# Written MLP order of a two-layer decoder trunk: another ring for the fourth weight piece, the first product copied ahead of the next step's splits, the turned blocks split ahead of two weight pieces

## The chip, the cores and the metric

The kernel runs on one core of one Trainium2 chip, as one program. The metric is device time in microseconds (us). TensorE (PE in the profile) multiplies, VectorE (DVE) and ScalarE (ACT) do the elementwise work, GpSimd (POOL) and SyncE (SP) mostly issue DMAs here.

## The reference

Two decoder layers over 256 tokens of width 2048, batch 1, everything in float32. Each layer has a token mixer and memory attention, and ends with a squared-ReLU MLP of inner width 8192:

```python
hm = _rmsnorm(x, g_mlp[i])
x = x + jnp.square(jax.nn.relu(hm @ w_mlp1[i])) @ w_mlp2[i]
```

The change touches the MLP alone. `w_mlp1` is 2048 x 8192 and `w_mlp2` is 8192 x 2048, both float32, so each layer reads 134 MB of MLP weights.

## The kernel before

**Exact products by halves.** TensorE multiplies in fp32r. Every weight and activation is split into a high part (ScalarE, `activation Copy` into fp32r, line 114) and a low part (VectorE, source minus high part, line 115). A product is three matmuls: high x high, high x low, low x high (`passes`, lines 606 to 608).

**How the MLP is tiled.** The 8192 inner columns are eight chunks `c` of 1024. The up projection of a chunk is done as a fast 2x2 block product with seven products (`p1` to `p7`, of which the trace prints only the letter `p`) instead of eight. It takes eight *steps* `kp`, each over 256 of the 2048 rows. A step loads two 512 KB pieces, `b` and `o` (lines 221 and 223), forms their sums on VectorE (`s` at line 226, then lines 230 and 232 overwrite halves of `o`), splits them into `bh/bl`, `oh`, `sh/sl`, `th/tl`, and runs 7 x 3 = 21 matmuls. After step 7, `end_up(c)` copies the first product out of PSUM (`c1`, line 655; the trace calls it `t`), combines the seven sums on VectorE into four blocks `u` (lines 656 to 664) and squares them on ScalarE (lines 611 and 612).

`to_hT(c)` turns the four blocks on TensorE (line 677, tile `pu`) and splits them into `hT`. `group_down(c, n, t)` is then 24 matmuls into `psd`, over eight pieces `dw`; the four 512 KB weight loads of one `n` (named by `k` = 0, 2, 4, 6) serve the two groups `t` = 0 and 1. `add_down` scales `psd` into `part` (line 699) and adds it to `x_sb` in SBUF by an accumulating GpSimd DMA (line 700).

**What sets the order.** The MLP loop stands inside `tc.manual_schedule()`: on each engine, instructions run in the order in which the Python emits them. For chunk `c` and `g` = 0 to 7 the loop emits: the matmuls of step `g`+1 of chunk `c+1` (for `g` = 7: of step 0 of chunk `c+2`); the loads and splits of the step after that one (`prep`); for odd `g`, loads and splits of the first two weight pieces of the next `n` (`prep_down(*more, (0,))`); a down group; its `add_down`; for odd `g`, the last two pieces (`prep_down(*more, (1,))`). At `g` = 0, `to_hT(c)` is interleaved with the step's products: block, `p1`, block, `p3` and `p2`, block, `p5` and `p7`, block, `p6` and `p4`. At `g` = 6, `end_up(c+1)` is emitted after `prep`.

**Rings.** All weight loads go through SP's one in-order queue; a load waits there until its buffer is free, and everything behind it waits too. The `raw` ring for down weights has three buffers (`RAW = 3`), so the fourth piece of an `n` waits until the first piece of the same `n` is split. The `ux` ring for `b` and `o` has five (`UX = 5`), of which two steps take four. The split pieces of a step have seven buffers (`UP = 7`), one step's worth, so ScalarE can start splitting for a step only when TensorE has used the same piece of the step before.

**PSUM.** Eight banks. A chunk's seven products hold seven of them until `end_up` has read them. The `pu` blocks and the `psd` groups share the eighth, one after the other.

Of the kernel before, what the change touches and what calls it, by code (L numbers as in the profile page):

```python
# [9 lines left out]
F32 = mybir.dt.float32  # L10
# [3 lines left out]
AF = mybir.ActivationFunctionType  # L14
# [3 lines left out]
P = 128  # L18
# [16 lines left out]
UX = 5  # L35
UT = 2
UP = 7
RAW = 3
# [20 lines left out]
def trunk(ctx: ExitStack, tc: tile.TileContext, x, mem, g_attn, w_in, w_out, lambda_qk,  # L59
          subln_g, g_mem, w_mem_kv, g_mlp, w_mlp1, w_mlp2, g_final, out):  # L60
    nc = tc.nc
# [3 lines left out]
    wpool = ctx.enter_context(tc.tile_pool(name="wpool", bufs=3))  # L65
    apool = ctx.enter_context(tc.tile_pool(name="apool", bufs=10))
    upool = ctx.enter_context(tc.tile_pool(name="upool", bufs=1))
# [4 lines left out]
    def bank(shape, nm, gemm=False):  # L72

        return psum.tile(shape, F32, tag="m" if gemm else "a", name=nm)
# [1 line left out]

    x_sb = const.tile([P, 2, D], F32, name="x_sb")

    def load_weights(src, k, c, nm):

        raw = wpool.tile([P, 1024], F32, tag="raw", bufs=RAW, name=f"raw_{nm}")
        nc.sync.dma_start(raw.rearrange("p (k c) -> p k c", c=c), src.rearrange("(k p) c -> p k c", p=P))
        return raw

# [28 lines left out]
    def split(dst_hi, dst_lo, src):  # L113
        nc.scalar.activation(dst_hi, src, AF.Copy)  # L114
        nc.vector.tensor_tensor(dst_lo, src, dst_hi.bitcast(F32), op=ALU.subtract)  # L115

    def weights(src, k, c, nm, raw=None):

        if raw is None:
            raw = load_weights(src, k, c, nm)  # L120
        hi = wpool.tile([P, 1024], F32R, tag="whi", bufs=WH, name=f"hi_{nm}")
        lo = wpool.tile([P, 1024], F32R, tag="wlo", bufs=WH, name=f"lo_{nm}")
        split(hi, lo, raw)
        return [(hi[:, kk * c:(kk + 1) * c], lo[:, kk * c:(kk + 1) * c]) for kk in range(k)]

    def gemm_feat(w, acts, nm, raws=(None,) * 4):

        ps = [bank([P, 2, 256], f"ps_{nm}_{j}", True) for j in range(2)]
        for pc in range(4):
            wt = weights(w[pc * 512:(pc + 1) * 512, :], 4, 256, f"{nm}_{pc}", raws[pc])  # L130
            for kk in range(4):
                k = 4 * pc + kk
                hi, lo = wt[kk]
                a = acts[k // 4][:, k % 4]
                for j in range(2):
                    last = k == KT - 1
                    cols = slice(j * P, (j + 1) * P)

                    def low(**f):
                        nc.tensor.matmul(ps[j][:, 0, :], lo[:, cols], a[:, 0, :], **f)  # L140

                    def high(**f):
                        nc.tensor.matmul(ps[j].rearrange("p h t -> p (h t)"), hi[:, cols], a.rearrange("p h t -> p (h t)"), **f)  # L143

                    if last:
                        low(start=False, stop=False)
                        high(start=False, stop=True)
                    else:
                        high(start=(k == 0), stop=False)
                        low(start=False, stop=False)  # L150
        return ps
# [14 lines left out]
    def act_tile(nm):  # L166
        return apool.tile([P, 4, 2, S], F32R, tag="act", name=nm)
# [270 lines left out]
    for i in range(DEPTH):  # L438
# [12 lines left out]
        for c in range(2):  # L451
            f0 = 3 * MIXW + c * 256
            ps = ps_first if i == c == 0 else gemm_feat(wi[:, f0:f0 + 256], xT, f"qm{i}{c}")
# [16 lines left out]
        for pr in range(NH // 2):  # L470
            ps = gemm_feat(wi[:, pr * 256:(pr + 1) * 256], xT, f"q{i}{pr}")
# [3 lines left out]
            ps = gemm_feat(wi[:, MIXW + pr * 256:MIXW + (pr + 1) * 256], xT, f"k{i}{pr}")  # L475
            aT2 = upool.tile([P, 2, 384], F32, tag="up", bufs=UP, name=f"aT{i}{pr}")
            feat_scaled(kT, ps, 1.0, rowb, f"k{i}{pr}")
            for j in range(2):
                h = 2 * pr + j
                nm = f"{i}_{h}"  # L480
# [99 lines left out]
        for c in range(4):  # L580
            ps = [bank([P, 512], f"pso{i}{c}_{t}", True) for t in range(2)]
            for n, g in enumerate(("m", 0, 1, 2)):
                r0 = MIXW if g == "m" else g * 512
# [13 lines left out]
        NC = DFF // 1024  # L597
# [7 lines left out]
        def passes(ps, acts, hi, lo, first, last):  # L605
            nc.tensor.matmul(ps, acts[:, 0, :], hi, start=first, stop=False)  # L606
            nc.tensor.matmul(ps, acts[:, 0, :], lo, start=False, stop=False)  # L607
            nc.tensor.matmul(ps, acts[:, 1, :], hi, start=False, stop=last)  # L608

        def squared(u, src, sign):  # L610
            nc.scalar.activation(u, src, AF.Relu, scale=sign)
            nc.scalar.activation(u, u, AF.Square)
# [16 lines left out]
        banks, facts, dw = {}, {}, {}  # L629
# [9 lines left out]
        def step_up(c, kp, turns=None, prep=None):  # L639

            if kp == 0:
                banks[c] = {n: bank([P, 512], f"{n}_{i}{c}", n in ("p1", "p2", "p5", "p7")) for n in facts[c, 0]}
            for n, (hi, lo) in facts.pop((c, kp)).items():
                if turns and n in ("p1", "p3", "p5", "p6"):
                    next(turns)
                    if n in ("p1", "p5"):
                        next(prep)
                passes(banks[c][n], comb[kp][:, FACTORS.index(n)], hi, lo, kp == 0, kp == KP - 1)

        def end_up(c):  # L650

            nm, ps = f"{i}{c}", banks.pop(c)
            c1, u2, u3, u4 = (work.tile([P, 512], F32, tag="tmp", bufs=TMP, name=f"t{n}_{nm}") for n in range(4))
            c11, m12, c21, m22 = (work.tile([P, 512], F32, tag="ev", bufs=EV, name=f"u{n}_{nm}") for n in range(4))
            nc.scalar.activation(c1, ps["p1"], AF.Copy)  # L655
            nc.vector.tensor_tensor(c11, c1, ps["p2"], op=ALU.add)
            nc.vector.tensor_tensor(u2, c1, ps["p6"], op=ALU.subtract)
            squared(c11, c11, 1.0)
            nc.vector.tensor_tensor(u4, u2, ps["p5"], op=ALU.add)
            nc.vector.tensor_tensor(m12, u4, ps["p3"], op=ALU.add)  # L660
            squared(m12, m12, -1.0)
            nc.vector.tensor_tensor(u3, u2, ps["p7"], op=ALU.add)
            nc.vector.tensor_tensor(m22, u3, ps["p5"], op=ALU.add)
            nc.vector.tensor_tensor(c21, u3, ps["p4"], op=ALU.add)
            yield
            squared(m22, m22, -1.0)
            squared(c21, c21, 1.0)
            ublk[c] = ((c11, 0, 0), (m12, 0, 1), (c21, 1, 0), (m22, 1, 1))

        def to_hT(c):  # L670

            for f in range(2):
                hT[f] = act_tile(f"hT{i}{c}{f}")
            for n, (u, t, f) in enumerate(ublk[c]):
                pt = bank([P, 4, P], f"pu_{i}{c}{n}")
                for k in range(4):
                    nc.tensor.transpose(pt[:, k], u[:, k * P:(k + 1) * P], ident)  # L677
                cols = slice(t * P, (t + 1) * P)
                split(hT[f][:, :, 0, cols], hT[f][:, :, 1, cols], pt)
                yield  # L680

        def prep_down(c, n, halves):

            for h in halves:
                for k in (4 * h, 4 * h + 2):
                    r0 = c * 1024 + k * P
                    dw[c, n, k], dw[c, n, k + 1] = weights(w_mlp2[i][r0:r0 + 256, n * 512:(n + 1) * 512], 2, 512,
                                                           f"d{i}{c}{n}{k}")

        def group_down(c, n, t, gemm):  # L690

# [34 lines left out]
        def run(steps):  # L726
            for _ in steps:
                pass

        up_plain()  # L730
        with tc.manual_schedule():
            run(prep_up(1, 0))
            step_up(1, 0)
            run(prep_up(1, 1))
            prep_down(0, 0, (0, 1))
            for c in range(NC - 1):
                for g in range(8):
                    uc, kp = (c + 1, g + 1) if g < 7 else (c + 2, 0)
                    pc, pk = (c + 1, g + 2) if g < 6 else (c + 2, g - 6)
                    prep = prep_up(pc, pk) if pc < NC else iter(())  # L740
                    if g == 0:
                        step_up(uc, kp, to_hT(c), prep)
                    elif uc < NC:
                        step_up(uc, kp)
                    run(prep)
                    ending = end_up(c + 1) if g == 6 else iter(())
                    next(ending, None)
                    n, t = g // 2, g % 2
                    more = (c, n + 1) if n < 3 else (c + 1, 0)
                    if t == 1:  # L750
                        prep_down(*more, (0,))
                    add_down(c, n, t, group_down(c, n, t, False))
                    run(ending)
                    if t == 1:
                        prep_down(*more, (1,))
            run(to_hT(NC - 1))
        last_down(NC - 1)
        xT = nxt
# [6 lines left out]
    for f in range(2):  # L765
        r0 = DFF - 1024 + f * 512
# [61 lines left out]
```

## Time and profile before

| | us |
|---|---|
| median of 3 runs (lowest, highest) | 2529.24 (2524.58, 2531.04) |
| the profiled execution | 2528.95 |
| its span, first to last instruction | 2527.2 |

| engine | busy us | share of the span |
|---|---|---|
| TensorE, matmuls | 2262.8 | 90% |
| VectorE | 1718.1 | 68% |
| ScalarE | 1334.0 | 53% |
| GpSimd | 115.8 | 5% |

The profile gives one execution. Its page has the busy share in 40 slices of the span; the trace behind it can be asked for the instructions of one engine in order of time (each with the idle time before it and what ended that), for the sum of waits by who waited for whom, and for the busy time and granted TensorE clock of any stretch. The two MLP loops run from about 518 to 1270 us and from about 1717 to 2470 us. A matmul's printed duration is its latency; matmuls overlap, so the distance between two starts is what one costs.

### The profile page before, as it was taken

Reading aid. Unit: us, or ns where it says so; the run is one execution under the profiler, and the core shown is the slowest. Engines: PE = TensorE matmul, PEld = TensorE weight load, DVE = VectorE, ACT = ScalarE, POOL = GpSimd, SP = SyncE. Lnnn points to the kernel's source line nnn. Section 1 sums busy time; section 2 is a strip of 40 time slices with the busy share of each in tenths; the row PEclk is TensorE's granted clock in tenths of the full one; section 3 lists DMA queues with packets and bytes.
Section 4 is the critical chain, followed back from the end, with each engine's and each line's share of the span. In section 5 each row is a group of like instructions: output and inputs, shape, how many; then the busy total and the mean of one; then the engine's idle time right before and its main releaser. Section 6 shows DMA issues by size and latency. Waiting matters only on the chain.

```text
span 2527.2 us, 28282 instructions
## 1 busy us (share of the span) xinstructions
PE 2262.8 (90%) x10358; PEld 1842.7 (73%) x10358; DVE 1718.1 (68%) x2084; ACT 1334.0 (53%) x1840; POOL 115.8 (5%) x146
## 2 busy tenths in 40 slices
PE   9999999988879788797999999998787978879797
PEld 7888887866757566575778888886675756657676
DVE  6567766667677677676766655766767767767675
ACT  7455554645455555555555544554545555555554
POOL 0000000000000000000000000000000000000000
PEclk9999999999989889898999999999998989989899
DMA  7655555645655565654655556564565556565465
GB/s 236 191 175 167 160 179 174 186 151 157 197 171 166 164 196 156 192 180 150 187 163 187 167 175 192 183 187 149 158 195 167 167 158 200 154 191 183 150 193 161
DMA packets 262397, 443.48 MB, mean 175 GB/s; under 512 B 14497, under 2 KB 80242, under 8 KB 262002
## 3 DMA queue, kind: packets, MB, share of 16 engines
q1 hardware_dynamic: 245856, 412.14, 50.5%
q0 software_dynamic: 16128, 29.37, 6.5%
q8 instruction: 81, 1.33, 0.2%
q14 instruction: 58, 0.48, 0.1%
q10 hardware_dynamic: 274, 0.17, 0.0%
HBM read 409.12 MB, written 3.15 MB: 163 GB/s over the span
## 4 chain that ended last, share of the span: by engine, by line
PE 53%; DVE 16%; DMA 16%; ACT 7%; issue 7%; SPq 1%; DVEq 0%; ACTq 0%; POOL 0%; POOLq 0%
DMA o<-in_w_mlp_dram 11%; DVE bl L115 4%; DMA raw_d<-in_w_mlp_dram 4%; PE ps_q L143 4%; PE ps_k L143 4%; ACT th L114 4%; PE psd L606 3%; PE psd L608 3%; PE psd L607 3%; DVE lo_d L115 3%; PE p L607 3%; PE p L606 2%; PE p L608 2%; PE pso L163 2%; PE pso L164 2%
## 5 line engine op out<-in xcount | busy, mean ns | idle before, releaser
L115 DVE TENSOR_TENSOR lo_d<-raw_d,hi_d 128x1024 fp32r<-128x1024 f32 x252 | 300.3, 1222 | 241.0 <-ACT hi_d L114 240.7
L606 PE MATMUL psd<-hi_d,hT 128*128 128x512 f32 x1008 | 395.5, 393 | 10.3 <-ACT hT L114 9.9
L607 PE MATMUL psd<-lo_d,hT 128*128 128x512 f32 x1008 | 394.2, 391 | 0.0
L608 PE MATMUL psd<-hi_d,hT 128*128 128x512 f32 x1008 | 393.2, 391 | 0.0
L114 ACT ACTIVATE hi_d<-raw_d 128x1024 fp32r<-128x1024 f32 x252 | 260.1, 1051 | 220.4 <-DMA raw_d<-in_w_mlp_dram 213.6
L606 PEld LDWEIGHTS psd<-hi_d,hT 128*128 128x128 f32 x1008 | 190.0, 189 | 56.8 <-ACT hT L114 11.4
L114 ACT ACTIVATE th<-o 128x1024 fp32r<-128x1024 f32 x112 | 118.8, 1061 | 196.7 <-DVE o L232 175.8
L608 PEld LDWEIGHTS psd<-hi_d,hT 128*128 128x128 f32 x1008 | 189.9, 188 | 40.4 <-DVE hT L115 0.6
L607 PEld LDWEIGHTS psd<-lo_d,hT 128*128 128x128 f32 x1008 | 190.2, 189 | 39.0
L226 DVE TENSOR_TENSOR s<-b,o 128x1024 f32<-128x1024 f32 x112 | 136.9, 1222 | 90.6 <-DMA o<-in_w_mlp_dram 90.6
L115 DVE TENSOR_TENSOR bl<-b,bh 128x1024 fp32r<-128x1024 f32 x112 | 136.8, 1221 | 87.8 <-ACT bh L114 87.8
L606 PE MATMUL p<-bh,cb_xm 128*128 128x512 f32 x224 | 105.1, 469 | 70.4 <-ACT t L655 66.6
L700 POOL DMA_DIRECT2D x_sb<-part x112 | 97.4, 869 | 1495.2 <-ACT part L699 1495.2
L677 PE MATMUL pu<-ident,u 128*128 128x128 f32 x256 | 50.8, 338 | 128.0 <-DVE hT L115 101.9
L677 PEld LDWEIGHTS pu<-ident,u 128*128 128x128 f32 x256 | 36.6, 172 | 149.3 <-DVE hT L115 114.7
L114 ACT ACTIVATE sh<-s 128x1024 fp32r<-128x1024 f32 x112 | 118.5, 1058 | 46.1 <-DVE s L226 39.7
L115 DVE TENSOR_TENSOR tl<-o,th 128x1024 fp32r<-128x1024 f32 x112 | 137.2, 1225 | 5.9 <-ACT th L114 0.3
L114 ACT ACTIVATE bh<-b 128x1024 fp32r<-128x1024 f32 x112 | 118.2, 1055 | 39.0 <-DMA b<-in_w_mlp_dram 32.8
L143 PE MATMUL ps_q<-xT,hi_q 128*128 128x512 f32 x384 | 138.4, 401 | 0.0
L143 PE MATMUL ps_k<-xT,hi_k 128*128 128x512 f32 x384 | 138.0, 399 | 0.0
L115 DVE TENSOR_TENSOR sl<-s,sh 128x1024 fp32r<-128x1024 f32 x112 | 136.5, 1218 | 0.0
L607 PE MATMUL p<-bl,cb_xm 128*128 128x512 f32 x224 | 100.0, 446 | 31.3 <-DVE bl L115 31.3
(331 smaller groups left out, 5174.7 us busy)
## 6 DMA issues: line engine op xcount, KB each, us to landing
raw_d<-in_w_mlp_dram SPq DMA_DIRECT2D x252, 512.0 KB, 9.1
b<-in_w_mlp_dram SPq DMA_DIRECT2D x112, 512.0 KB, 9.1
o<-in_w_mlp_dram SPq DMA_DIRECT2D x112, 512.0 KB, 9.9
x_sb<-part POOLq DMA_DIRECT2D x112, 256.0 KB, 5.3
raw_q<-in_w_in_dram SPq DMA_DIRECT2D x48, 512.0 KB, 3.7
raw_k<-in_w_in_dram SPq DMA_DIRECT2D x48, 512.0 KB, 3.6
raw_v<-in_w_in_dram SPq DMA_DIRECT2D x48, 512.0 KB, 3.7
raw_o<-in_w_out_dram SPq DMA_DIRECT2D x48, 512.0 KB, 3.7
```

The lines of the kernel that those rows point to most:

```text
L114: nc.scalar.activation(dst_hi, src, AF.Copy)
L115: nc.vector.tensor_tensor(dst_lo, src, dst_hi.bitcast(F32), op=ALU.subtract)
L143: nc.tensor.matmul(ps[j].rearrange("p h t -> p (h t)"), hi[:, cols], a.rearrange("p h t -> p (h t)"), **f)
L163: nc.tensor.matmul(ps[t], ah, lo, start=False, stop=False)
L164: nc.tensor.matmul(ps[t], al, hi, start=False, stop=last and kk == 3)
L226: nc.vector.tensor_tensor(s, b, o[:, 0:1].to_broadcast([P, 2, 512]), op=ALU.add)
L606: nc.tensor.matmul(ps, acts[:, 0, :], hi, start=first, stop=False)
L607: nc.tensor.matmul(ps, acts[:, 0, :], lo, start=False, stop=False)
L608: nc.tensor.matmul(ps, acts[:, 1, :], hi, start=False, stop=last)
L677: nc.tensor.transpose(pt[:, k], u[:, k * P:(k + 1) * P], ident)
L700: nc.gpsimd.dma_start(x_sb[:, t, n * 512:(n + 1) * 512], part, accum_op=ALU.add)
```

## The change

Three edits, in the MLP's written order and its loads. `load_weights` can take its buffer from the `ux` ring, and `prep_down` does so for the piece `k` = 6. `end_up` gives control back right after the copy `c1`, and the loop calls that part before `prep`. At `g` = 7 the last two weight pieces of the next chunk are no longer prepared after the group; they are prepared at the next `g` = 0, after the step and its `to_hT`. The same holds ahead of the first chunk.

```diff
-    def load_weights(src, k, c, nm):
-
-        raw = wpool.tile([P, 1024], F32, tag="raw", bufs=RAW, name=f"raw_{nm}")
+    def load_weights(src, k, c, nm, other=False):
+
+        if other:
+            raw = upool.tile([P, 1024], F32, tag="ux", bufs=UX, name=f"raw_{nm}")
+        else:
+            raw = wpool.tile([P, 1024], F32, tag="raw", bufs=RAW, name=f"raw_{nm}")
...
             c1, u2, u3, u4 = (work.tile([P, 512], F32, tag="tmp", bufs=TMP, name=f"t{n}_{nm}") for n in range(4))
+            nc.scalar.activation(c1, ps["p1"], AF.Copy)
+            yield
             c11, m12, c21, m22 = (work.tile([P, 512], F32, tag="ev", bufs=EV, name=f"u{n}_{nm}") for n in range(4))
-            nc.scalar.activation(c1, ps["p1"], AF.Copy)
...
-                    dw[c, n, k], dw[c, n, k + 1] = weights(w_mlp2[i][r0:r0 + 256, n * 512:(n + 1) * 512], 2, 512,
-                                                           f"d{i}{c}{n}{k}")
+                    w, nm = w_mlp2[i][r0:r0 + 256, n * 512:(n + 1) * 512], f"d{i}{c}{n}{k}"
+                    dw[c, n, k], dw[c, n, k + 1] = weights(w, 2, 512, nm, load_weights(w, 2, 512, nm, k == 6))
...
-            prep_down(0, 0, (0, 1))
+            prep_down(0, 0, (0,))
...
                     if g == 0:
                         step_up(uc, kp, to_hT(c), prep)
+                        prep_down(c, 0, (1,))
                     elif uc < NC:
                         step_up(uc, kp)
+                    ending = end_up(c + 1) if g == 6 else iter(())
+                    next(ending, None)
                     run(prep)
-                    ending = end_up(c + 1) if g == 6 else iter(())
                     next(ending, None)
...
-                    if t == 1:
+                    if t == 1 and n < 3:
                         prep_down(*more, (1,))
+            prep_down(NC - 1, 0, (1,))
             run(to_hT(NC - 1))
```

ScalarE, layer 0, at `g` = 6 of chunk 4. `hi_d` are the last two weight pieces of `n` = 3, `t<-p` is the copy `c1`, and `bh`, `oh`, `sh`, `th` are the splits for step 0 of chunk 6. Before:

```order
L114 ACTIVATE hi_d_8105<-raw_d_8103 128x1024
L114 ACTIVATE hi_d_8111<-raw_d_8109 128x1024
L114 ACTIVATE bh_8143<-b_8136 128x1024
L114 ACTIVATE oh_8141<-o_8138 128x512
L114 ACTIVATE sh_8151<-s_8140 128x1024
L114 ACTIVATE th_8155<-o_8138 128x1024
L655 ACTIVATE t_05_8159<-p_05_7478 128x512
L611 ACTIVATE u_05_8163<-u_05_8163 128x512
```

The copy stands behind the four splits. After:

```order
L117 ACTIVATE hi_d_8105<-raw_d_8103 128x1024
L117 ACTIVATE hi_d_8111<-raw_d_8109 128x1024
L657 ACTIVATE t_05_8136<-p_05_7478 128x512
L117 ACTIVATE bh_8148<-b_8141 128x1024
L117 ACTIVATE oh_8146<-o_8143 128x512
L117 ACTIVATE sh_8156<-s_8145 128x1024
L117 ACTIVATE th_8160<-o_8143 128x1024
L614 ACTIVATE u_05_8164<-u_05_8164 128x512
```

The copy stands ahead of them; nothing else moved here.

VectorE, layer 0, around `to_hT(5)`. `lo_d` are the low parts of the four weight pieces of the next `n` = 0, `hT` the low parts of the four turned blocks, `s` and `bl` belong to the next step. Before:

```order
L115 TENSOR_TENSOR lo_d_7532<-raw_d_7529,hi_d_7531 128x1024
L115 TENSOR_TENSOR lo_d_7538<-raw_d_7535,hi_d_7537 128x1024
L115 TENSOR_TENSOR lo_d_7572<-raw_d_7569,hi_d_7571 128x1024
L115 TENSOR_TENSOR lo_d_7578<-raw_d_7575,hi_d_7577 128x1024
L115 TENSOR_TENSOR hT_7581<-pu_7583,hT_7581 128x4x128
L226 TENSOR_TENSOR s_7594<-b_7590,o_7592 128x1024
L115 TENSOR_TENSOR hT_7582<-pu_7600,hT_7582 128x4x128
L115 TENSOR_TENSOR hT_7581<-pu_7613,hT_7581 128x4x128
L115 TENSOR_TENSOR bl_7621<-b_7590,bh_7620 128x1024
L115 TENSOR_TENSOR hT_7582<-pu_7630,hT_7582 128x4x128
L230 TENSOR_TENSOR o_7592<-s_7594,b_7590 128x512
```

All four weight pieces stand ahead of the first turned block. After:

```order
L118 TENSOR_TENSOR lo_d_7532<-raw_d_7529,hi_d_7531 128x1024
L118 TENSOR_TENSOR lo_d_7538<-raw_d_7535,hi_d_7537 128x1024
L118 TENSOR_TENSOR hT_7569<-pu_7571,hT_7569 128x4x128
L229 TENSOR_TENSOR s_7582<-b_7578,o_7580 128x1024
L118 TENSOR_TENSOR hT_7570<-pu_7588,hT_7570 128x4x128
L118 TENSOR_TENSOR hT_7569<-pu_7601,hT_7569 128x4x128
L118 TENSOR_TENSOR bl_7609<-b_7578,bh_7608 128x1024
L118 TENSOR_TENSOR hT_7570<-pu_7618,hT_7570 128x4x128
L118 TENSOR_TENSOR lo_d_7634<-raw_d_7631,hi_d_7633 128x1024
L118 TENSOR_TENSOR lo_d_7640<-raw_d_7637,hi_d_7639 128x1024
L233 TENSOR_TENSOR o_7580<-s_7582,b_7578 128x512
```

Two pieces now stand behind the turned blocks, and ahead of the rest of the step's sums.

SP's queue at the same kind of place (the next `n` = 0 of chunk 2). `raw_d` are the weight pieces, `b` and `o` a step's. Before:

```order
L82 DMA raw_d_6063<-in_w_mlp_dram 128x2x512
L82 DMA raw_d_6069<-in_w_mlp_dram 128x2x512
L82 DMA raw_d_6103<-in_w_mlp_dram 128x2x512
L82 DMA raw_d_6109<-in_w_mlp_dram 128x2x512
L221 DMA b_6124<-in_w_mlp_dram 128x2x512
L223 DMA o_6126<-in_w_mlp_dram 128x2x512
```

After:

```order
L85 DMA raw_d_6063<-in_w_mlp_dram 128x2x512
L85 DMA raw_d_6069<-in_w_mlp_dram 128x2x512
L224 DMA b_6112<-in_w_mlp_dram 128x2x512
L226 DMA o_6114<-in_w_mlp_dram 128x2x512
L85 DMA raw_d_6165<-in_w_mlp_dram 128x2x512
L85 DMA raw_d_6171<-in_w_mlp_dram 128x2x512
```

Two step loads pass two weight loads there. Everywhere else in the loop SP's order is the same, and what differs is the buffer that the fourth piece goes to: before it took the buffer of the first piece of its own `n`, now one that was last read a pair of steps earlier. The loads of `b` and `o` now also wait for readers one pair of steps earlier (`bh` on ScalarE and `tl` on VectorE). TensorE's order in the loop is unchanged.

## Rows read from the trace of the kernel before

**Rows 1.** The page: busy time by engine.

```profile
PE 2262.8 (90%) x10358; PEld 1842.7 (73%) x10358; DVE 1718.1 (68%) x2084; ACT 1334.0 (53%) x1840; POOL 115.8 (5%) x146
```

**Rows 2.** Stretches: start and end, length, busy time by engine (with instructions), granted TensorE clock, DMA share, GB/s. The first is one period of the loop in layer 0, from one start of step `g` = 6 to the next, the second the stage between the two MLPs, the last two six such periods of each layer.

```profile
815.40:924.20 108.80, 91.20 (x377) 72.36 (x376) 78.97 (x84) 57.86 (x70) 6.93 (x8) 0.92 0.57 174
1278.00:1720.00 442.00, 439.57 (x2264) 373.07 (x2262) 266.44 (x359) 231.77 (x363) 1.41 (x2) 1.00 0.57 174
...
599.10:1250.00 650.90, 545.01 (x2257) 432.69 (x2256) 470.40 (x499) 344.61 (x414) 41.56 (x48) 0.91 0.57 175
1798.00:2450.00 652.00, 547.51 (x2255) 434.38 (x2254) 469.93 (x498) 344.50 (x414) 41.64 (x48) 0.91 0.57 174
```

**Rows 3.** TensorE in order of time (start, duration, tile, idle time before and what ended it): one `to_hT` and the first matmul of the first group, then the first matmul of steps `g` = 1, 2 and 6, then the next `to_hT` (of the first `to_hT` the first, third and fourth block are shown, of the next the first).

```profile
847.18 0.66 PE L677 MATMUL pu<-ident,u 128*128 128x128 f32 x4 [1.83 <-ACT part L699]
...
858.51 0.66 PE L677 MATMUL pu<-ident,u 128*128 128x128 f32 x4
...
860.59 0.66 PE L677 MATMUL pu<-ident,u 128*128 128x128 f32 x4
...
862.67 0.50 PE L606 MATMUL psd<-hi_d,hT 128*128 128x512 f32 x1
...
868.24 0.39 PE L606 MATMUL p<-bh,cb_xm 128*128 128x512 f32 x1
...
878.44 0.39 PE L606 MATMUL p<-bh,cb_xm 128*128 128x512 f32 x1
...
924.25 0.39 PE L606 MATMUL p<-bh,cb_xm 128*128 128x512 f32 x1
...
955.77 0.66 PE L677 MATMUL pu<-ident,u 128*128 128x128 f32 x4 [1.50 <-ACT part L699]
```

**Rows 4.** Who TensorE waited for in the one period of rows 2 (total us, times, longest).

```profile
PE pu L677 <- DVE hT L115: 6.7, 1, 6.7
PE p L606 <- ACT t L655: 6.0, 1, 6.0
PE p L607 <- DVE bl L115: 2.2, 1, 2.2
PE pu L677 <- ACT part L699: 1.8, 1, 1.8
```

**Rows 5.** SP's queue in order of issue over one pair of steps (a row that is merged, x4, spans from its first to its last issue).

```profile
877.40 0.37 SPq L82 DMA_DIRECT2D raw_d<-in_w_mlp_dram  x1
...
880.12 20.88 SPq L82 DMA_DIRECT2D raw_d<-in_w_mlp_dram  x4
```

**Rows 6.** What ScalarE and VectorE waited for over six periods of layer 0 (599 to 1250 us).

```profile
ACT hi_d L114 <- DMA raw_d<-in_w_mlp_dram: 84.4, 24, 4.5
...
DVE s L226 <- DMA o<-in_w_mlp_dram: 40.7, 24, 3.0
```

**Rows 7.** VectorE in order of time: the end of one pair's weight pieces, and then `g` = 6 (the fourth piece, the next step's first sum, two of the `u` operations).

```profile
876.15 2.35 DVE L115 TENSOR_TENSOR lo_d<-raw_d,hi_d 128x1024 fp32r<-128x1024 f32 x2
...
930.41 1.23 DVE L115 TENSOR_TENSOR lo_d<-raw_d,hi_d 128x1024 fp32r<-128x1024 f32 x1 [3.06 <-ACT hi_d L114]
934.35 1.23 DVE L226 TENSOR_TENSOR s<-b,o 128x1024 f32<-128x1024 f32 x1 [2.71 <-DMA o<-in_w_mlp_dram]
...
941.56 0.68 DVE L657 TENSOR_TENSOR t<-t,p 128x512 f32<-128x512 f32 x1
...
943.60 0.68 DVE L662 TENSOR_TENSOR t<-t,p 128x512 f32<-128x512 f32 x1
```

**Rows 8.** ScalarE in order of time at `g` = 6 of the same chunk (third and fourth weight piece, copy `c1`), and then the fourth piece ahead of the last `to_hT` of layer 0.

```profile
925.04 1.05 ACT L114 ACTIVATE hi_d<-raw_d 128x1024 fp32r<-128x1024 f32 x1
929.32 1.06 ACT L114 ACTIVATE hi_d<-raw_d 128x1024 fp32r<-128x1024 f32 x1 [3.23 <-DMA raw_d<-in_w_mlp_dram]
...
939.69 0.58 ACT L655 ACTIVATE t<-p 128x512 f32<-128x512 f32 x1
...
1271.06 1.06 ACT L114 ACTIVATE hi_d<-raw_d 128x1024 fp32r<-128x1024 f32 x1 [3.23 <-DMA raw_d<-in_w_mlp_dram]
```

**Rows 9.** DMA issues on the page: line, count, size, median us from issue to landing, of the MLP's three loads and of one that comes in the stage between the MLPs.

```profile
raw_d<-in_w_mlp_dram SPq DMA_DIRECT2D x252, 512.0 KB, 9.1
...
o<-in_w_mlp_dram SPq DMA_DIRECT2D x112, 512.0 KB, 9.9
...
raw_q<-in_w_in_dram SPq DMA_DIRECT2D x48, 512.0 KB, 3.7
```

**Rows 10.** The first `to_hT` of layer 0, TensorE and VectorE in order of time: first block, VectorE's first three weight pieces, second block, the first matmul of the first group, and that of step `g` = 6 of that chunk.

```profile
517.77 0.60 PE L677 MATMUL pu<-ident,u 128*128 128x128 f32 x4
...
521.23 3.49 DVE L115 TENSOR_TENSOR lo_d<-raw_d,hi_d 128x1024 fp32r<-128x1024 f32 x3
...
530.54 1.12 PE L677 MATMUL pu<-ident,u 128*128 128x128 f32 x4 [11.48 <-DVE hT L115]
...
538.06 0.50 PE L606 MATMUL psd<-hi_d,hT 128*128 128x512 f32 x1
...
599.10 0.39 PE L606 MATMUL p<-bh,cb_xm 128*128 128x512 f32 x1
```

**Rows 11.** Two stretches of 3 us, after the burst of issues that begins in rows 5 and later in the same pair (columns as in rows 2; the last is GB/s).

```profile
889.00:892.00 3.00, 2.43 (x12) 1.69 (x11) 2.92 (x5) 1.46 (x2) 0.00 (x0) 1.00 1.03 390
895.00:898.00 3.00, 3.00 (x15) 2.49 (x14) 2.97 (x5) 1.00 (x2) 0.00 (x0) 1.00 0.14 24
```

## The prediction

> **What bounds the kernel now.** I began with the busy shares [rows 1]: TensorE is at 90% and no other engine above 68%, but that is a mean over stages. By stretches [rows 2], TensorE has no idle time worth naming between the two MLPs (439.57 of 442 us, clock 1.00). In an MLP period of 108.8 us it is busy 91.2 us and its clock is granted at 0.92. So the loss lies in the MLP loops: six periods take 650.9 us in layer 0 and 652.0 us in layer 1.
>
> How little could a period take? A step with its group is 45 matmuls, and the starts of steps 1 and 2 are 878.44 - 868.24 = 10.20 us apart with no wait between [rows 3], or 0.227 us a matmul: 4.76 us a step, 5.44 us a group. Eight are 81.6 us, and the four turned blocks add about 2 (estimate: 0.66 us each [rows 3], partly overlapped). That is 83.6 us. VectorE has 79.0 us of work in the period and ScalarE 57.9 [rows 2], so TensorE is the floor, with VectorE close behind it.
>
> Who does TensorE wait for [rows 4]? 6.7 us for the low part of the first turned block, 6.0 us for the copy `c1`, 2.2 us for `bl`, and 1.8 us for `part`: 16.7 us. The other 108.8 - 83.6 - 16.7 = 8.5 us agree with the clock: 8% of 108.8 us is 8.7 us, lost at the lower of the two levels, 1.2 instead of 2.4 GHz.
>
> All four waits are late elementwise work, and the queue and the two elementwise engines show why it is late [rows 5 to 8]. SP issues the fourth weight piece at 877.40 us [rows 5], just as the low part of that group's first piece ends (876.15 plus half of 2.35 us [rows 7]); the next fourth piece, last of the merged row, goes out at 880.12 + 20.88 - 0.37 = 900.63. A pair of steps thus takes 23.2 us, against 20.4 us of matmuls. ScalarE waits for a weight DMA 24 times in six periods, 84.4 us in all, and VectorE for the step's `o`, queued behind it on SP, 24 times, 40.7 us [rows 6]. That is once in each pair. The elementwise engines lose three to five us on TensorE there, and it pays at `c1` and at `to_hT`.
>
> **The fourth piece in the steps' ring.** It goes to a buffer last read one pair earlier, so SP no longer stops in mid-pair. The price is that `b` and `o` now wait for readers one pair earlier. On a 20.4 us pair the latest of these, `o` of an odd step, is free after the low part `tl` of that step and wanted when VectorE forms `s` for the same step of the next pair. Setting the row durations one behind the other gives some 12.6 us between (estimate). The loads land 9.1 to 9.9 us after issue in today's bursts, 3.7 us when they come singly [rows 9]. I take their waits as gone, and count what follows in three stretches of the period.
>
> *Steps 1 to 5 and their groups*: 924.25 - 868.24 = 56.0 us now [rows 3], 5 x 10.20 = 51.0 us if TensorE sets the pace. VectorE's work for a pair, two steps at some 6.6 us and four low parts at 1.15 us, is about 18 us of 20.4. Gain 5.0 us.
>
> *Step 6 to the next `to_hT`*: 955.77 - 924.25 = 31.5 us now [rows 3]. VectorE starts the next step's `s` at 934.35 [rows 7], and from there to the first turned block is 955.77 - 934.35 = 21.4 us of splits, `u` blocks, squares, splits, two weight pieces and `part`, with no load waited for. Unstalled, ScalarE makes the third high part at 925.04 [rows 8], the fourth right behind it, VectorE its low part, and `s` can start near 928.4, 4.15 us after step 6 instead of 10.1. So 4.15 + 21.4 = 25.6 us: gain 5.9. TensorE has 20.4 us of work here and so still waits about 5 us, split in two: about 1.9 in step 7's products (the bank for `p3` is free after line 657, 7.9 us into VectorE's chain, that for `p5` after line 662, 10 us into it [rows 7]), about 3.3 ahead of the first turned block.
>
> **The first product copied first.** ScalarE has the copy at 939.69, 5.34 us after `s` [rows 7, 8]. With `s` at 4.15 us it would end at 10.1 us even in the old order, as step 7 begins (10.2). So this edit alone is worth nothing to half a us, and the products behind it wait for line 657 on VectorE. It adds a wait of ScalarE for step 6's `p1`, with the four splits queued behind; `p1` is done 0.7 us into step 6, ScalarE gets there at 2.9 us, so it costs nothing. Were ScalarE ahead of TensorE, it would wait there at most until `p1` is done, and step 7 comes 10.2 us after step 6.
>
> **The turned blocks ahead of two weight pieces.** From the first block to step 1 now takes 868.24 - 847.18 = 21.1 us [rows 3]. Each block must be turned, copied and split before the next can have its bank, and an undisturbed link takes 860.59 - 858.51 = 2.08 us, as does the last, to 862.67 [rows 3]. After the change only two weight pieces stand ahead, which end while the first block is turned. Four links are 8.3 us, the group 5.6 (868.24 - 862.67): 13.9 us, gain 7.2. Some 3.5 us of it is the load wait (84.4 / 24 [rows 6]), 2.4 us this edit (two low parts at 1.15 us), the rest the clock. The moved pieces end about 2.3 us into the group, which reaches the last of them after 18 x 0.227 = 4.1 us, and the next step's sums behind them on VectorE end 2 us ahead of need. So they cost nothing; without that cover, up to 2.3 us a period. Two step loads pass two weight loads on SP, both long before use.
>
> **The clock.** A period is thus 25.6 + 13.9 + 51.0 = 90.5 us, from 31.5 + 21.1 + 56.0 = 108.6. No row shows the clock in the new pattern, so I bound its cost by none and by today's 8.5 us. The longest wait left is 3.3 us, where 6.7, 6.0 and 2.2 stand now: in proportion 8.5 x 3.3 / 14.9, about 1.8 us. I take 1.7, nearer to none, since both waits over 5 us go: 92.2 us, gain 16.4.
>
> **The sum.** Twelve periods: 12 x 16.4 = 196.8 us. The first chunk of each layer, from its first turned block to step 6: 599.10 - 517.77 = 81.3 us now [rows 10]. After it, the second block waits for two weight pieces (521.23 + 2 x 1.16) and one split of 0.7, until 524.3, 6.5 us after the first; three links 6.2, group 5.6, five steps 51.0, clock 1.7: 71.0. Gain 10.3, twice 20.6. At the end of each layer the wait of 3.23 us for the fourth piece [rows 8] goes: 6.4. Nothing else in the program is idle enough to gain. Together 223.8 us. The profiled execution took 2528.95 us, 0.3 us below the median, so 2528.95 - 223.8 = **2305 us**, 8.9% less.
>
> **Rivals.** *The clock stays as bad.* The remaining 3.3 us and the links keep the lower level in every period: 12 x 6.8 = 82 us back, 2387 us. For it: a period has waits either way. Against it: 16.7 us of long waits shrink to about 7 in small ones.
>
> *A wait takes the place of the one removed.* If loads of `b` and `o` come some 3 us too late in each pair, because their buffers are free only one pair ahead, steps 1 to 5 gain nothing and the chain to `to_hT` half of it: about 8 us a period back, 2400 us. It needs a landing time of some 16 us against 12.6; today's longest medians are 9.9.
>
> *The loads themselves bound it, and it gets slower.* A period needs 32 loads. Issued one by one as buffers come free, each taking its 3.7 us alone [rows 9] without overlap, they would take 118 us, 9.6 us more than now: 12 x 9.6 = 115 us, 2644 us. It decides from 108.6 / 32 = 3.4 us a load. Against it: within today's burst the queue moved 390 GB/s, or 1.35 us a load, and 24 GB/s later in the pair [rows 11]; 174 GB/s, 3.0 us a load, go along with a TensorE without waits between the MLPs [rows 2]. The forecast needs 2.9 us a load (92.2 / 32).
>
> The Trainium skill speaks against loads of this size ("DMA: Bandwidth & Descriptors", section "Bandwidth"): it asks for at least 1 MiB a transfer and measures 341 GB/s there and 138 GB/s at 64 KB. At its lower figure 32 loads would take an estimated 122 us, at the upper 49 us. The 390 GB/s of these half-size loads lie above both, so the measurement decides against that rule here as long as several are queued.
>
> *The change doesn't do what it says.* If the fourth piece still waited, say for a `tl` that ends as late as today's first low part, only the two reorderings would be left: 14 x 2.4 us, 2495 us.
>
> **How the numbers follow.** Forecast 0.75, the clock as bad 0.12, the replaced wait 0.06, no effect of the ring 0.02, the loads as bound 0.03, no measurable change 0.02. With the clock at none in all 14 stretches the forecast gives 2281 us; if the wait ahead of the turned blocks also shrinks by one us in each period, 2269. The other end is the clock rival, 2387. The range is 2268 to 2388. A measurement of this kernel can tell about 0.3%, 7.6 us, from no change. Faster by more 0.95, within 0.02, slower 0.03.
>
> **What would show it.** In the profile after: ScalarE's waits for weight DMAs and VectorE's for `o` near zero; steps 1 to 5 at 10.2 us each; no wait of TensorE for `c1`, but one to two us for line 657; three to four us for `part` ahead of the turned blocks, then links of 2.1 us; a period of 90 to 94 us and a clock of at least 0.96 over six of them. It is wrong if pairs stay over 21 us, if VectorE waits for loads, or if the clock stays near 0.91.

## The result, and the profile after

| | before | after |
|---|---|---|
| median, us | 2529.59 | 2299.95 |
| lowest, highest, us | 2524.58, 2531.04 | 2299.35, 2300.86 |
| span of the profiled execution, us | 2527.2 | 2297.6 |

The kernel before was run once more, which moves its median from 2529.24 to 2529.59. The changed kernel takes 0.9096 of the time before, 95% interval 0.908 to 0.9111: 9.0% faster, 5 us below the forecast of 2305. I read its profile in the order in which the one of before was read. First the page's busy time by engine, against [rows 1]:

```profile
PE 2207.4 (96%) x10358; PEld 1814.3 (79%) x10358; DVE 1715.9 (75%) x2084; ACT 1332.0 (58%) x1840; POOL 115.4 (5%) x146
```

VectorE and ScalarE have the same work as before; only the span they share is shorter. Next, stretches with the columns of [rows 2]: one period split at its first turned block, step 1, step 6 and the next first turned block, then the six periods of each layer, from step 6 to step 6.

```profile
885.81:901.50 15.69, 15.49 (x61) 11.83 (x62) 11.38 (x13) 7.69 (x10) 0.86 (x1) 0.81 0.56 166
901.50:952.50 51.00, 51.00 (x226) 42.23 (x225) 45.61 (x47) 31.66 (x36) 4.33 (x5) 1.00 0.78 231
952.50:978.07 25.57, 21.12 (x91) 16.51 (x89) 21.29 (x26) 18.01 (x24) 1.75 (x2) 0.98 0.61 179
585.82:1136.93 551.11, 522.07 (x2257) 420.92 (x2256) 469.72 (x499) 344.15 (x414) 41.53 (x48) 0.97 0.69 203
1672.97:2223.04 550.07, 521.03 (x2257) 419.71 (x2256) 469.78 (x499) 344.10 (x414) 41.60 (x48) 0.98 0.69 203
```

The columns are start and end, length, busy time of TensorE, weight loads, VectorE, ScalarE and GpSimd with their instructions, granted clock, DMA share and GB/s. The same three stretches took 21.06, 56.0 and 31.5 us before [rows 3]. In steps 1 to 5 TensorE is now busy all the time at clock 1.00. A period is 551.11 / 6 = 91.9 us in layer 0 and 91.7 in layer 1; the forecast said 92.2.

Who TensorE waits for in the period that begins at 885.81 (total us, times, longest), the whole answer, against [rows 4]:

```profile
PE pu L681 <- ACT part L703: 2.9, 1, 2.9
PE p L609 <- DVE t L661: 1.1, 1, 1.1
PE p L609 <- ACT u L614: 0.5, 1, 0.5
```

16.7 us of waits have become 4.5, and all of them lie between the start of step 7 and the first turned block. Lines have moved by 3 or 4: 661 was 657. The same place in order of time on TensorE: the two waits of step 7, and the turned blocks with some of the products between them.

```profile
964.60 0.50 PE L609 MATMUL p<-bh,cb_xm 128*128 128x512 f32 x1 [1.05 <-DVE t L661]
...
966.73 0.47 PE L609 MATMUL p<-sh,cb_xm 128*128 128x512 f32 x1 [0.48 <-ACT u L614]
...
978.07 1.12 PE L681 MATMUL pu<-ident,u 128*128 128x128 f32 x4 [2.92 <-ACT part L703]
...
979.41 0.63 PE L610 MATMUL p<-bl,cb_xm 128*128 128x512 f32 x1
979.84 0.63 PE L611 MATMUL p<-bh,cb_xm 128*128 128x512 f32 x1
980.60 1.11 PE L681 MATMUL pu<-ident,u 128*128 128x128 f32 x4
...
984.05 0.60 PE L681 MATMUL pu<-ident,u 128*128 128x128 f32 x4
...
984.73 0.39 PE L610 MATMUL p<-sl,cb_xm 128*128 128x512 f32 x1
984.96 0.39 PE L611 MATMUL p<-sh,cb_xm 128*128 128x512 f32 x1
...
986.07 0.66 PE L681 MATMUL pu<-ident,u 128*128 128x128 f32 x4
```

After the wait of 2.92 us the matmuls start 0.43 us apart (979.41, 979.84), and from 984.73 on 0.23 us. The first links (from one turned block to the next) take 2.53 and 3.45 us, the third 2.02. The granted clock at the start and at the end of these links is that of 1.2 GHz, then that of 2.4 (columns as above):

```profile
978.07:980.60 2.53, 2.40 (x7) 1.58 (x8) 1.76 (x3) 0.60 (x1) 0.85 (x1) 0.50 0.88 274
984.40:988.15 3.75, 3.67 (x19) 2.48 (x17) 2.52 (x3) 2.93 (x4) 0.00 (x0) 1.00 0.08 31
```

The wait is the same in the other periods, but not the clock behind it. The stretch from the first turned block to step 1, 15.69 us in the period above, takes 13.87 to 15.70 us in the twelve periods of the two layers, 15.20 in the mean. The shortest:

```profile
2067.00:2080.87 13.87, 13.05 (x62) 9.81 (x62) 11.40 (x13) 7.71 (x10) 0.87 (x1) 1.00 0.64 183
...
2067.00 0.66 PE L681 MATMUL pu<-ident,u 128*128 128x128 f32 x4 [2.89 <-ACT part L703]
2069.07 0.66 PE L681 MATMUL pu<-ident,u 128*128 128x128 f32 x4 [0.72 <-DVE hT L118]
```

What ScalarE and VectorE wait for over six periods (588 to 1131 us), the first rows of each answer, against [rows 6]:

```profile
ACT th L117 <- DVE o L235: 80.0, 47, 2.0
ACT part L703 <- PE psd L611: 37.9, 29, 1.7
ACT hT L117 <- PE pu L681: 33.8, 24, 2.5
...
DVE lo_d L118 <- ACT hi_d L117: 33.9, 24, 1.8
```

Neither answer has a row that names a DMA; 84.4 and 40.7 us stood there. SP's queue over one pair of steps, against [rows 5], and one row of VectorE:

```profile
909.53 0.37 SPq L226 DMA_DIRECT2D o<-in_w_mlp_dram  x1
910.67 5.66 SPq L85 DMA_DIRECT2D raw_d<-in_w_mlp_dram  x4
...
931.06 5.67 SPq L85 DMA_DIRECT2D raw_d<-in_w_mlp_dram  x4
...
922.47 1.22 DVE L229 TENSOR_TENSOR s<-b,o 128x1024 f32<-128x1024 f32 x1
```

The four weight pieces of a pair go out within 5.66 us instead of 20.88, and the queue's pair takes 931.06 - 910.67 = 20.4 us instead of 23.2: the queue keeps TensorE's pace. The `o` issued at 909.53 is wanted by the `s` at 922.47, 12.9 us later (the prediction put this at 12.6). The DMA issues of layer 0's six periods (count, size, median us from issue to landing), against [rows 9]:

```profile
raw_d<-in_w_mlp_dram SPq DMA_DIRECT2D x96, 512.0 KB, 5.8
```

The `b` loads land in 4.4 us and the `o` loads in 3.7. In the six periods before, the three medians were 9.8, 7.9 and 10.1 us.

### The profile page after: what moved, and what is told of

Read it like the earlier page. It is cut to its first block, busy times and chain, and to the rows that moved or that the text cites. A ratio compares the mean times of both kernels' runs of the same rounds, so it can differ in the third digit from the quotient of the medians.

```text
span 2297.6 us, 28469 instructions
## 1 busy us (share of the span) xinstructions
PE 2207.4 (96%) x10358; PEld 1814.3 (79%) x10358; DVE 1715.9 (75%) x2084; ACT 1332.0 (58%) x1840; POOL 115.4 (5%) x146
## 4 chain that ended last, share of the span: by engine, by line
PE 83%; DVE 8%; ACT 6%; issue 3%; DMA 0%; ACTq 0%; DVEq 0%; SPq 0%; POOL 0%; POOLq 0%
PE psd L609 8%; PE psd L611 8%; PE psd L610 8%; PE p L609 6%; PE p L610 6%; PE p L611 6%; PE ps_q L146 4%; PE ps_k L146 4%; PE pso L166 2%; PE pso L167 2%; PE pso L165 2%; PE ps_k L143 2%; PE ps_q L143 2%; PE psv L166 2%; PE psv L167 2%
## 5 line engine op out<-in xcount | busy, mean ns | idle before, releaser
L117 ACT ACTIVATE hi_d<-raw_d 128x1024 fp32r<-128x1024 f32 x252 | 256.9, 1051 | 14.2 <-PE psd L611 5.8
L703 ACT ACTIVATE part<-psd,rsq 128x512 f32<-128x512 f32 x112 | 76.8, 686 | 99.5 <-PE psd L611 97.6
L609 PE MATMUL p<-bh,cb_xm 128*128 128x512 f32 x224 | 96.7, 432 | 12.7 <-DVE t L661 12.7
L143 PE MATMUL ps_q<-xT,lo_q 128*128 128x256 f32 x384 | 107.1, 284 | 0.0
L143 PE MATMUL ps_k<-xT,lo_k 128*128 128x256 f32 x384 | 106.7, 283 | 0.0
```

Of the source, the lines that this page charges most:

```text
L703: nc.scalar.activation(part, ps, AF.Copy, scale=rsq[:, t:t + 1])
```

## Experiments

Two theories ran through them. T1 is the prediction's: the ring takes the load wait out of every pair, the turned blocks save what stood ahead of them, the copy is worth nothing. T2 credits the orders with more: the wait for `c1` is TensorE's second largest, so ending it early should pay, with the ring or alone. All ratios are to the kernel before, run on the same chip (medians 2528.65 us for the first four runs, 2528.71 for the last three).

### The ring alone

Before, with only this of the change:

```diff
+        if other:
+            raw = upool.tile([P, 1024], F32, tag="ux", bufs=UX, name=f"raw_{nm}")
...
+                    dw[c, n, k], dw[c, n, k + 1] = weights(w, 2, 512, nm, load_weights(w, 2, 512, nm, k == 6))
```

> Only the fourth weight piece moves to the steps' ring; the copy and the turned blocks stay where they were. Theory 1 (the stop in the load queue is what cost, the orders are small): the pairs run at 20.4 us, the turned blocks queue behind two more low parts, 2.4 us a period, the copy costs 0 to 0.5 us: 2300 + 14 x 2.4 to 2.9 = 2334 to 2341 us. Theory 2 (the waits named for the copy and the turned blocks are made by their places in the written order): 6.0 and 6.7 us a period remain, only the 2.2 us wait and the pair's slack go: about 2460 us.

Measured: 2330.11 us, 0.9214 [0.92, 0.9227], 4 us (0.2%) below T1's range and far from T2's 2460. One period, split as above:

```profile
893.50:910.43 16.93, 15.13 (x61) 11.57 (x62) 13.62 (x15) 7.59 (x10) 0.86 (x1) 0.80 0.64 203
910.43:961.43 51.00, 51.00 (x226) 42.23 (x225) 43.23 (x44) 31.61 (x35) 4.33 (x5) 1.00 0.74 214
961.43:987.00 25.57, 21.23 (x92) 16.40 (x90) 21.28 (x26) 18.07 (x25) 1.75 (x2) 1.00 0.61 179
```

The second and third stretch are those of the whole change to 0.01 us. Only the first is longer, so the ring alone accounts for steps 1 to 7, with the copy still behind the splits. It gains 2528.65 - 2330.11 = 198.5 us, or 14.2 in each of 14 stretches; the prediction's shares for it, without the clock, are 5.0 + 5.9 + 3.5 = 14.4.

### The ring and the copy

The whole change, with all four weight pieces ahead of the turned blocks again:

```diff
-            prep_down(0, 0, (0,))
+            prep_down(0, 0, (0, 1))
...
-                        prep_down(c, 0, (1,))
...
-                    if t == 1 and n < 3:
+                    if t == 1:
...
-            prep_down(NC - 1, 0, (1,))
```

> Ring and copy, turned blocks behind all four weight pieces as before. Theory 1: 2.4 us a period more than with all three, 2300 + 14 x 2.4 = 2334 us. Theory 2: the 6.7 us wait at the turned blocks stays, 2380 to 2395 us.

Measured: 2331.23 us, 0.9219 [0.9205, 0.9232]. The copy adds nothing to the ring: T1.

### The ring and the turned blocks

The whole change, with the copy back at its old place:

```diff
-            nc.scalar.activation(c1, ps["p1"], AF.Copy)
-            yield
...
+            nc.scalar.activation(c1, ps["p1"], AF.Copy)
...
-                    ending = end_up(c + 1) if g == 6 else iter(())
-                    next(ending, None)
                     run(prep)
+                    ending = end_up(c + 1) if g == 6 else iter(())
```

> Ring and turned blocks, the copy behind the four splits as before. Theory 1: the copy ends at 10.1 us after step 6 where step 7 needs it at 10.2, and the products behind it wait for VectorE anyway: 2300 to 2307 us. Theory 2: the copy's 6.0 us a period come back, 2300 + 14 x 6 = 2384 us.

Measured: 2301.17 us, 0.9097 [0.9084, 0.9111], the time of the whole change. T1.

### Both orders without the ring

The whole change, with the fourth piece back in the `raw` ring:

```diff
-weights(w, 2, 512, nm, load_weights(w, 2, 512, nm, k == 6))
+weights(w, 2, 512, nm, load_weights(w, 2, 512, nm))
```

> Both orders, no change of ring: the fourth piece still waits for the first of its own group. Theory 1: pairs stay at 23 to 24 us; at the turned blocks the load wait now lies beside them, so 2.4 to 6.5 us a period are gained: 2438 to 2495 us. Theory 2: both named waits go, 2529 - 14 x 12 = 2361 us.

Measured: 2429.09 us, 0.9605 [0.9589, 0.9621]. It lies below T1's range and far above T2's: neither expected it. One period, split as before:

```profile
823.31:838.38 15.07, 14.29 (x61) 11.08 (x62) 11.39 (x13) 7.70 (x10) 0.86 (x1) 0.89 0.74 219
838.38:894.38 56.00, 53.23 (x227) 43.20 (x225) 44.33 (x46) 31.51 (x36) 4.32 (x5) 0.97 0.59 176
894.38:926.17 31.79, 23.77 (x91) 18.32 (x90) 22.84 (x27) 18.34 (x24) 1.74 (x2) 0.84 0.58 182
```

The last two stretches are as long as before the change, and the first is as short as with it. The stop of the load queue stays, as T1 said: SP issues the `b` behind the fourth piece at 847.97, 871.19 and 895.15 us, 23.2 and 24.0 us apart. Why the first stretch is short all the same, ScalarE shows in order of time in this period: the third and fourth weight piece of the pair with the turned blocks, and then those of the next pair.

```profile
831.92 2.00 ACT L117 ACTIVATE hi_d<-raw_d 128x1024 fp32r<-128x1024 f32 x2
...
849.37 1.05 ACT L117 ACTIVATE hi_d<-raw_d 128x1024 fp32r<-128x1024 f32 x1
852.01 1.06 ACT L117 ACTIVATE hi_d<-raw_d 128x1024 fp32r<-128x1024 f32 x1 [1.59 <-DMA raw_d<-in_w_mlp_dram]
```

The first two run back to back, with no wait. Before, ScalarE waited 4.15 us for the fourth piece there, and the low part of the first turned block came behind it:

```profile
852.22 1.06 ACT L114 ACTIVATE hi_d<-raw_d 128x1024 fp32r<-128x1024 f32 x1 [4.15 <-DMA raw_d<-in_w_mlp_dram]
```

The other three waits of the period stay (1.59, 4.47 and 3.34 us). So preparing the last two pieces after the turned blocks takes away not only the two low parts that I had counted but the load wait of that pair too. The edit moves the loads, the high parts and the low parts together; no run moved one of them alone.

### The copy alone

Before, with the copy ahead of the splits and nothing else:

```diff
+            nc.scalar.activation(c1, ps["p1"], AF.Copy)
+            yield
...
-            nc.scalar.activation(c1, ps["p1"], AF.Copy)
...
+                    ending = end_up(c + 1) if g == 6 else iter(())
+                    next(ending, None)
                     run(prep)
-                    ending = end_up(c + 1) if g == 6 else iter(())
```

> The copy alone, ring and turned blocks as before. Theory 1: TensorE's wait for the copy turns into a wait for VectorE's line that frees the next bank; three matmuls move ahead, 0 to 0.7 us a period: 2519 to 2529 us. Theory 2: the 6.0 us wait goes, 2445 us.

Measured: 2529.68 us, 1.0002 [0.9991, 1.0012]: no change. TensorE's waits in one period of it (844 to 953 us), the whole answer, against [rows 4]:

```profile
PE pu L681 <- DVE hT L118: 5.6, 1, 5.6
PE p L609 <- DVE t L661: 4.8, 1, 4.8
PE p L610 <- DVE bl L118: 4.5, 2, 2.3
PE pu L681 <- ACT part L703: 2.1, 1, 2.1
PE p L610 <- DVE sl L118: 1.1, 2, 0.7
```

No row names the copy any more. The product that waited 6.0 us for `c1` now starts on time, and the next waits 4.8 us for line 661 on VectorE. This run and the one before it differ in the turned edit only, which without the ring is thus worth 2529.68 - 2429.09 = 100.6 us.

### Four buffers in each ring

The whole change, with all pieces in `raw` and one buffer moved from ring to ring:

```diff
-UX = 5
+UX = 4
-RAW = 3
+RAW = 4
...
-weights(w, 2, 512, nm, load_weights(w, 2, 512, nm, k == 6))
+weights(w, 2, 512, nm, load_weights(w, 2, 512, nm))
```

> All of the change, but the fourth piece goes to a fourth buffer of its own ring, and the steps' ring has four instead of five buffers. Theory 1 (what matters is that the buffer was last read a pair earlier, in whichever ring): the same waits in the queue, 2293 to 2307 us. Rival (the fifth buffer of the steps' ring gives slack that the pieces share): loads of b and o come late, over 2320 us.

Measured: 2295.47 us, 0.9081 [0.9066, 0.9096]; its interval overlaps that of the change. What counts is that the fourth piece doesn't wait for the first of its own `n`. Which of the two rings has the buffer makes no difference that these runs can tell, and the steps need no fifth.

### The high parts of two pieces made earlier

The wait left is that for `part`, which ScalarE makes late. This kernel is the whole change, and for the first `n` of a chunk ScalarE makes the high parts of the first two pieces ahead of the last split of `g` = 7; VectorE makes the second low part after the first turned block, and the step's `s` after the second.

```diff
+        if mid:
+            mid()
...
+        def high_first(c):
...
+                nc.scalar.activation(hi, raw, AF.Copy)
...
+            def low():
+                lo, raw, hi = made.pop(0)
+                nc.vector.tensor_tensor(lo, raw, hi.bitcast(F32), op=ALU.subtract)
...
+                    ahead = g == 7 and pc < NC
...
+                    if ahead:
+                        late[0]()
```

> All of the change, and at the end of a chunk the high parts of the first two weight pieces are written on ScalarE ahead of the step's last split, where it idles 1.8 us for VectorE, and the second low part and the next step's first sum stand behind the first and the second turned block on VectorE. Theory 1 (the chain of ScalarE and VectorE up to the psd copy ends the 2.9 us wait, and TensorE has slack behind it): part comes 1.9 us earlier, the links of the turned blocks run without the lower clock: 1.9 to 3.3 us a period, 12 periods, 2260 to 2277 us. Rival (the wait is bound by TensorE's own group and the copy of its sum): no change, 2293 to 2307 us.

Measured: 2267.58 us, 0.8968 [0.8954, 0.8983], in T1's range and faster than both kernels. One period, split as before, and TensorE's turned blocks in it:

```profile
941.43:965.08 23.65, 21.12 (x92) 16.52 (x90) 19.39 (x24) 17.90 (x24) 1.75 (x2) 1.00 0.64 191
965.08:979.30 14.22, 13.06 (x61) 9.81 (x62) 13.19 (x15) 7.69 (x10) 0.85 (x1) 1.00 0.66 192
979.30:1030.30 51.00, 51.00 (x226) 42.23 (x225) 45.62 (x47) 31.64 (x36) 4.32 (x5) 1.00 0.79 229
...
965.08 0.66 PE L685 MATMUL pu<-ident,u 128*128 128x128 f32 x4 [0.99 <-ACT part L730]
967.50 0.66 PE L685 MATMUL pu<-ident,u 128*128 128x128 f32 x4 [1.07 <-DVE hT L118]
969.57 0.66 PE L685 MATMUL pu<-ident,u 128*128 128x128 f32 x4
```

The first row is the stretch from step 6 to the first turned block, the third row above. The wait for `part` falls from 2.92 to 0.99 us and this stretch from 25.57 to 23.65, as much as the wait lost. The stretch behind it takes 14.22 us at clock 1.00, with one link of 2.42 us and others of 2.07. That is so in ten of twelve periods. In the other two the clock falls behind nearly the same wait (0.95 us ahead of this one):

```profile
608.31:623.82 15.51, 14.38 (x61) 11.09 (x62) 13.23 (x15) 7.74 (x10) 0.87 (x1) 0.89 0.59 173
```

The twelve take 14.44 us in the mean, 0.76 less than with the change. So of the 2.7 us gained in a period, 1.92 are the wait and 0.76 lie behind it: the lower clock costs 0.2 us in the mean instead of 1.3, and the first link takes 0.35 us more (2.42 against 2.07).

## Why the prediction was right, and what it mis-sized

**Steps 1 to 5** were put at 51.0 us and took 51.00. The ring does it alone. The pair of 23.2 us was the load queue's: on TensorE steps 1, 3, 5 and 6 started at 868.24, 888.64, 909.95 and 924.25 before, so its pairs took 20.40 and 21.31 us and most of the loss lay in the one step from 5 to 6 (14.30). "Pairs over 21 us" was thus a weak sign of being wrong.

**Step 6 to the next `to_hT`** was put at 25.6 us and took 25.57. Its working holds too: VectorE starts the next step's `s` 4.15 us after step 6 (952.50).

```profile
956.65 1.22 DVE L229 TENSOR_TENSOR s<-b,o 128x1024 f32<-128x1024 f32 x1
```

Its 1.9 us of waits in step 7 came out as 1.05 + 0.48, its 3.3 ahead of the first turned block as 2.92. For the second wait of step 7 the profile names line 614 on ScalarE, not the line 662 of the forecast (now 666); line 666 ends at 966.58, 0.15 us before the product starts, and with the ring alone the profile names that line. The ring alone gives 25.57, so the copy has no part in it.

**The copy** was put at nothing to half a us a period. With the ring, adding it changed the whole run by 2331.23 - 2330.11 = +1.1 us, with the turned blocks too by 2299.95 - 2301.17 = -1.2, both inside the intervals; without the ring the ratio is 1.0002. The 6.0 us wait for it [rows 4] was real, but the instruction behind it in the same products waits for VectorE in any case.

**First block to step 1** was put at 13.9 us and 1.7 for the clock, 15.6. The twelve periods took 15.20 in the mean. The one at clock 1.00 took 13.87, so the 13.9 hold, and the clock cost 0 to 1.8 us, 1.3 in the mean. It sits in the links: in the period from 978.07 they take 10.08 us, to the group at 988.15, against the forecast's 8.3, and the group 5.59. The signs named for this place came out in part: the wait for `part` was just under three us, and the links kept 2.1 us only where the clock stayed up. I had no row for the term and scaled it by the longest wait (8.5 x 3.3 / 14.9 is 1.9, not 1.8). Waits of 2.88 to 2.92 us that cost anything from 0 to 1.8 don't bear out that rule, so that 1.7 came near was luck.

**The turned edit** was credited with the wrong share. I booked a gain of 7.2 us a period for this stretch, of which 3.5 to the ring, 2.4 to this edit, the rest to the clock. With the ring in place this edit is worth (2330.11 - 2301.17) / 14 = 2.1 us a period, close to 2.4. Without the ring it is worth 100.6 / 14 = 7.2, the whole of the stretch. Both edits remove the same load wait there. So the step that failed is in the rival in which the ring does nothing: it booked 2.4 us for the edit where 7.2 are measured, and its 2495 us should have been about 2429. The two alone sum to (2528.65 - 2330.11) + 100.6 = 299 us and together bring 229. The 70 us between, 5.0 a period, I read as that one wait (4.15 us in the period shown), with its clock, counted twice. The forecast escaped this only because it summed stretches of a period and not edits.

**The sum** by its terms, each as us gained in the two layers together (from the starts of the first turned block, of step 6 and of the last `to_hT` in both traces):

| term | predicted | measured |
|---|---|---|
| six periods, twice | 196.8 | 650.93 - 551.11 + 652.73 - 550.07 = 202.5 |
| first chunk, twice | 20.6 | 9.9 + 10.5 = 20.4 |
| from the last `to_hT` on, both layers | 6.4 | 0.65 + 2.73 = 3.4 |
| ahead of layer 0's first turned block | 0 | 517.77 - 514.38 = 3.4 |
| together | 223.8 | 229.6 |

The 5.7 us of the first row make up the difference: the mean of the twelve periods before is the 108.6 us that I worked from, but after it is 91.8, not 92.2. That is the clock term again, 1.3 us and not 1.7. At the layer's end the 3.23 us wait for the fourth piece [rows 8] goes, but the group behind the last `to_hT` then waits for the low part of a turned block. In order of time on TensorE, layer 0:

```profile
1155.89 0.50 PE L609 MATMUL psd<-hi_d,hT 128*128 128x512 f32 x1 [1.41 <-ACT hT L117]
...
1160.46 0.79 PE L611 MATMUL psd<-hi_d,hT 128*128 128x512 f32 x1 [2.87 <-DVE hT L118]
```

Two small misses cancel here, by luck: 3.0 us too much at the ends, 3.4 not foreseen at the start. The last is not shown to be the change's work: the first turned block of layer 0 starts anywhere from 512.42 to 517.55 us in the seven experiments, at 514.45 with the copy alone, which gains nothing, and at 517.55 with the ring and the turned blocks.

**The rivals.** The clock did not stay as bad: 0.97 over six periods. No wait took the place of the one removed: loads land in 3.7 to 5.8 us and the lead is 12.9. The loads did not bound: 32 of them in 92 us are 2.9 us each, less than one takes to land, so they overlap.

## What to carry to other kernels

Where one in-order queue feeds several rings, look for the load whose buffer is freed by work of its own group: it stops every load behind it, and one more buffer, from either ring here, freed them all. Sum a forecast by stretches of time and not by edits, because two edits can remove the same wait. A wait's length beside a name is not what removing that name is worth: ask what the next instruction waits for, and for 6.0 us the answer here was nothing.

## What the runs showed of the hardware

More bytes in a second went with shorter landings. Over six periods the DMA engines moved 203 GB/s and the 512 KB loads landed in medians of 3.7 to 5.8 us, where 175 GB/s had gone with 7.9 to 10.1. Before, SP issued the four step loads of a pair within 2 us (877.82, 878.33, 878.84 and 879.35); now they go out 3.0 to 3.8 us apart (899.11, 902.86, 905.82 and 909.53). No run changed the spacing alone.

A wait's length does not settle the clock behind it. Twelve waits of 2.88 to 2.92 us at the same place in the changed kernel went with a granted clock of 0.81 (six times), 0.88 to 0.89 (five) and 1.00 (once) up to step 1. Twelve of 0.93 to 1.00 us in the last experiment, where a second of about one us follows, went with 1.00 (ten times) and 0.89 (twice). So the clock fell behind eleven of the longer waits and behind two of the shorter; what decides in a single period stays open.
